# Prompt attention with TensorE's order written out: products of a unit in one run, scores and transposes in turn, exponentials over 1024 columns

## The chip, the cores and the metric

The kernel runs on one core of a Trainium2 chip. The metric is the time of one execution on the device in microseconds (us), the median of several runs. A core has five engines with a queue of instructions each: TensorE (PE in the profile, with its weight loads as PEld), VectorE (DVE), ScalarE (ACT), GpSimd (POOL) and SyncE (SP, which issues most DMAs). An engine works through its queue in order. Waits between engines are semaphores that the framework places from the data dependencies.

## The reference

One inference step of a decoder layer with two kinds of heads, for a prompt of 2048 tokens and for 64 sampled tokens with a paged cache. What matters here is the prompt's forgetting attention, 8 heads of 64 channels, all in float32:

```
L = jnp.cumsum(logf, axis=1).transpose(0, 2, 1)
s = jnp.einsum('bqhd,bkhd->bhqk', q_i, k).astype(jnp.float32) * scale
s = s + L_i[..., :, None] - L[:, :, None, :]
s = jnp.where(k_pos[None, :] <= q_pos[:, None], s, -jnp.inf)
p = jax.nn.softmax(s, axis=-1)
return jnp.einsum('bhqk,bkhd->bqhd', p.astype(v.dtype), v)
```

A query block of 128 rows `qt` (0 to 15) sees the (qt+1)*128 keys up to its own end. The rest of the step (input projection, mLSTM heads, attention over the cache, output projection, layer norms, squared-ReLU MLP) is not touched by the change.

## The kernel before, in words

The kernel is one program of consecutive phases. `phase_b` is the prompt attention; it lies between the input projection with the mLSTM heads and `phase_o`, the output projection. A framework collects the instructions with their dependencies and then decides, from a timeline of its own, in which order they stand on each engine. `tc.issue_after(x)` pins an instruction behind `x` in that order. The order in which the Python code creates instructions is a priority, not a rule.

`phase_b` runs over 64 *units* (h, g): 8 heads, and in each head 8 groups g of two query blocks, qt = 2g and 2g+1; the two blocks are the *halves* i = 0 and 1 of a unit. In step n of the loop the scores of unit n are made and then the values of unit n-1 (`LA = 1`).

`scores` (from L928): for each half the keys are taken in pieces of up to 512 columns. A piece is a *score pair* on PE: two matmuls into one PSUM bank `pS`, with the high part `qh` (L945) and the low part `ql` (L946) of the queries as weights and the keys `ks` streaming. Three banks `pS` take turns. DVE drains the bank into the SBUF tile `S`, adds the forget row `nl` and keeps the maximum (L952); the diagonal 128 columns are drained with the masked row `nd`, which POOL makes (L956). A small DVE reduction makes the row maximum `mx` (L959).

`values` (from L963): ACT takes the exponential in place, one instruction for each 512-column tile, with the row sum in `lp` (L973); DVE adds up `lp` (L974). Then, for every four key blocks, both halves are transposed: up to four 128x128 transposes on PE into a PSUM tile `pt` (L986, three buffers), and a copy of `pt` to SBUF tile `PT` by ACT (L989; half 0, and every second group of half 1) or DVE (L991). I call four such transposes and their copy a *turn*. After the turns of a group come the *value products* of these four key blocks (L995), which accumulate into `po`; a unit has 2g+2 products. In the trace one product leaves two records. At the end `po` is copied out by ACT (L1001) and its second half added by DVE (L1003); after every fourth unit `finish` normalises and stores.

The keys of the next head (`ks`, an ACT and a DVE instruction for each 512 columns, L154 and L157) and the next queries (`qh`, `ql`) are made between the two. `tick`, which feeds other work into some phases, has an infinite pace in this phase and starts nothing. `S` has ten buffers of 512 columns. The two statements of the loop that matter are:

```
sc[n] = scores(Z[h], g)
...
values(Z[h], g, sc.pop(n - LA))
```

Of the kernel before, what the change touches and what calls it, by code (L numbers as in the profile page):

```python
# [10 lines left out]
F32 = mybir.dt.float32  # L11
# [14 lines left out]
S = 2048  # L26
# [26 lines left out]
def body(ctx, tc, I, O, stages):  # L53
# [80 lines left out]
    def tick(us):  # L134

        macc[0] += us
        while macc[1] and macc[0] > macc[2]:
            macc[0] -= macc[2]
            if beside(macc[1][0]) == 0:
                macc[1].pop(0)  # L140
        if not macc[1]:
            macc[0] = 0.0
        acc[0] += us
        while acc[1] is not None and acc[0] > acc[2]:
            acc[0] -= acc[2]
            attend()
# [718 lines left out]
    def phase_b():  # L865
# [58 lines left out]
            split_lo(ql, qn, qh)  # L924
            z["q", g] = qh, ql

        def scores(z, g):

            qh, ql = z.pop(("q", g))
            nl, ks = z["nl"], z["ks"]  # L930
            out = []
            for i in range(2):
                qt = 2 * g + i
                n = (qt + 1) * 128
                qs = slice(i * 128, i * 128 + 128)
                mx = pb.tile([128, 8], F32, name="mx", bufs=6)
                nd = pb.tile([128, 128], F32, name="nd", bufs=3)
                last["POOL"] = G.tensor_tensor(nd, nl[:, qt * 128:n], dmask, op=OP.add)
                st = []
                j = 0  # L940
                for a in range(0, n, 512):
                    b = min(n, a + 512)
                    w = max(b - a, 256)
                    pS = bank()
                    T.matmul(pS[:, :w], qh[:, qs], ks[:, a:a + w], start=True, stop=False)  # L945
                    last["PE"] = T.matmul(pS[:, :w], ql[:, qs], ks[:, a:a + w], start=False, stop=True)  # L946
                    tick(0.42)
                    sp = pb.tile([128, 512], F32, name="S", bufs=10)
                    st.append(sp)
                    e = min(b, qt * 128)  # L950
                    if e > a:
                        last["DVE"] = V.tensor_tensor_reduce(out=sp[:, :e - a], in0=pS[:, :e - a], in1=nl[:, a:e], scale=1.0, scalar=NEG,  # L952
                                               op0=OP.add, op1=OP.max, accum_out=mx[:, j:j + 1])
                        j += 1
                    if b == n:
                        V.tensor_tensor_reduce(out=sp[:, e - a:b - a], in0=pS[:, e - a:b - a], in1=nd, scale=1.0, scalar=NEG,  # L956
                                               op0=OP.add, op1=OP.max, accum_out=mx[:, j:j + 1])
                        j += 1
                V.tensor_reduce(mx[:, 7:8], mx[:, :j], axis=AX.X, op=OP.max, negate=True)  # L959
                out.append((st, mx))  # L960
            return out

        def values(z, g, sc):  # L963

            if z["h"] == 0 and g == 0:
                pad(pb, 64)
            for i, (st, mx) in enumerate(sc):
                qt = 2 * g + i
                n = (qt + 1) * 128
                lp = pb.tile([128, 4], F32, name="lp", bufs=6)  # L970
                for k, sp in enumerate(st):
                    w = min(512, n - k * 512)
                    last["ACT"] = A.activation(sp[:, :w], sp[:, :w], AF.Exp, bias=mx[:, 7:8], accum_out=lp[:, k:k + 1])  # L973
                V.tensor_reduce(z["ls"][:, qt:qt + 1], lp[:, :len(st)], axis=AX.X, op=OP.add)  # L974

            po = ppb.tile([128, 256], F32, name="po", bufs=1)
            nk = 2 * g + 2
            for k0 in range(0, nk, 4):
                PT = pb.tile([128, 4, 256], F32, name="PT", bufs=4)
                for i in range(2):  # L980
                    kk = min(4, 2 * g + i + 1 - k0)
                    if kk <= 0:
                        continue
                    pt = ppb.tile([128, 4, 128], F32, name="pt", bufs=3)
                    for k in range(kk):
                        T.transpose(pt[:, k], sc[i][0][k0 // 4][:, k * 128:(k + 1) * 128], ident)  # L986
                    dst = PT[:, :kk, i * 128:i * 128 + 128]
                    if i == 0 or (k0 // 4) % 2 != 0:
                        A.copy(dst, pt[:, :kk])  # L989
                    else:  # L990
                        V.tensor_copy(dst, pt[:, :kk])  # L991
                for k in range(k0, min(k0 + 4, nk)):
                    q0 = 128 if k == nk - 1 else 0
                    c = (k % 2) * 64
                    last["PE"] = T.matmul(po[c:c + 64, q0:], z["vn"][:, k], PT[:, k - k0, q0:],  # L995
                                          start=(k < 2), stop=(k >= nk - 2), skip_group_check=True)
                tick(0.45 * min(4, nk - k0))
            if g % 4 == 0:
                z["ot"] = pb.tile([64, 1024], F32, name="ot", bufs=2)
            od = z["ot"][:, (g % 4) * 256:(g % 4) * 256 + 256]  # L1000
            A.copy(od, po[0:64])  # L1001
            q0 = 128 if g == 0 else 0
            V.tensor_tensor(od[:, q0:], od[:, q0:], po[64:128, q0:], op=OP.add)  # L1003
            if g % 4 == 3:
                finish(z, g // 4)
# [34 lines left out]
        for n in range(len(units) + LA):  # L1040
            if 10 <= n < 16 and acc[1] is not None:
                attend()
            w2_due[0] += 64 * (n % 8 // 2 + 1) / 150
            while n and len(w2_done) < min(64, w2_due[0]):
                w2_sum()
            if n == 60:
                wo.extend(half_wo(0, q) for q in range(4))
            if n < len(units):
                h, g = units[n]
                sc[n] = scores(Z[h], g)  # L1050
                if h == 0 and g % 2 == 0 and g < 6:
                    keys(Z[0], g // 2 + 1)
                if h < 7:
                    if g == 3:
                        Z[h + 1] = head(h + 1)
                        forget_values(Z[h + 1], 0, S)
                    if g >= 4:
                        keys(Z[h + 1], g - 4)
                if n + 1 < len(units):
                    queries(Z[units[n + 1][0]], units[n + 1][1])  # L1060
            if n >= LA:
                h, g = units[n - LA]
                values(Z[h], g, sc.pop(n - LA))
        es.close()


# [31 lines left out]
    def half_wo(hf, q):  # L1098

        r = raw().rearrange("p (k c) -> p k c", k=2)  # L1100
        SY.dma_start(r, I["w_o2"][hf, q].rearrange("p (k c) -> p k c", k=2))
        return r
# [800 lines left out]
```

## Time and profile before

| | |
|---|---|
| median of 3 runs | 3292.24 us (3286.64 to 3301.8) |
| the profiled execution, its own time | 3288.1 us |
| its span, first to last instruction | 3286.4 us |
| PE busy | 3148.6 us, 96% |
| DVE busy | 2099.1 us, 64% |
| ACT busy | 1500.7 us, 46% |
| POOL busy | 912.9 us, 28% |
| mean granted TensorE clock | 0.984 |

The profile is of one execution. Busy time on PE is the union of the matmuls' records; since matmuls are pipelined, a record goes on after the next one has begun, and a PE that is busy need not be at its peak rate. What an instruction costs its engine in a dense stretch is therefore read from start to start, not from its duration.

### The profile page before, as it was taken

How to read it: one execution, taken by the hardware profiler on the slowest of the kernel's cores; microseconds unless marked ns; L12 is line 12 of the kernel's file. 1: busy time of each engine (PE TensorE's matmuls, PEld its weight loads, DVE VectorE, ACT ScalarE, POOL GpSimd, SP SyncE). 2: the span in 40 equal slices, each digit the busy share in tenths (PEclk: the TensorE clock that was granted, in tenths of full speed). 3: DMA queues.
4: the chain of work that ended last, by engine and by line, in shares of the span. 5: the costliest groups of instructions: out<-in, count | busy, mean ns of one | idle time of the engine just before them, and what ended most of it. 6: DMA issues, size and time to landing. Idle time of an engine off the chain costs nothing.

```text
span 3286.4 us, 58046 instructions
## 1 busy us (share of the span) xinstructions
PE 3148.6 (96%) x21681; PEld 2564.4 (78%) x21681; DVE 2099.1 (64%) x5079; ACT 1500.7 (46%) x2966; POOL 912.9 (28%) x977
## 2 busy tenths in 40 slices
PE   8999998998989999999999999999999999799997
PEld 8998998888856666677677777776777777698895
DVE  6856565355468788644466658656586666856658
ACT  4343343233358888622344345343454444444442
POOL 0121233322324333276433422433333121100000
PEclk9999999999989999999999999999999999999998
DMA  5575766766678675487887878878879666543332
GB/s 186 149 221 177 236 221 216 236 232 198 223 232 226 160 201 136 159 298 253 305 292 273 290 256 298 315 254 327 289 290 343 218 231 211 187 152 119 120 105 100
DMA packets 339698, 734.37 MB, mean 223 GB/s; under 512 B 63640, under 2 KB 177688, under 8 KB 338520
## 3 DMA queue, kind: packets, MB, share of 16 engines
q1 hardware_dynamic: 252856, 416.71, 39.6%
q0 software_dynamic: 83520, 304.12, 26.6%
q10 hardware_dynamic: 3040, 9.83, 0.8%
q8 instruction: 171, 2.80, 0.3%
q14 instruction: 111, 0.91, 0.1%
HBM read 677.71 MB, written 86.38 MB: 233 GB/s over the span
## 4 chain that ended last, share of the span: by engine, by line
PE 45%; DVE 3%; DMA 3%; issue 1%; POOL 1%; ACT 1%; another core or an unknown queue 0%; DVEq 0%; POOLq 0%; ACTq 0%; SPq 0%
PE ph L162 7%; PE ph L163 7%; PE ph L164 7%; PE py L162 6%; PE py L164 5%; PE py L163 5%; PE sO L1759 3%; PE sQ L1647 2%; DMA vt<-cache_v,idxV 1%; DVE wl L157 1%; PE sT L1716 1%; DVE y L1323 1%; DMA kT<-cache_k,idxK 0%; PE pw L163 0%; PE pw L164 0%
## 5 line engine op out<-in xcount | busy, mean ns | idle before, releaser
L157 DVE TENSOR_TENSOR wl<-wr,wh 128x1024 fp32r<-128x1024 f32 x364 | 445.6, 1226 | 376.3 <-ACT wh L154 341.0
L154 ACT ACTIVATE wh<-wr 128x1024 fp32r<-128x1024 f32 x364 | 382.6, 1054 | 321.8 <-PE ph L163 131.1
L162 PE MATMUL ph<-x1h,wh 128*128 128x512 f32 (+1 forms) x1280 | 455.8, 356 | 0.8 <-DVE x1l L157 0.5
L163 PE MATMUL ph<-x1l,wh 128*128 128x512 f32 (+1 forms) x1280 | 453.9, 355 | 0.0
L1624 POOL DMA_INDIRECT kT<-cache_k,idxK x256 | 273.7, 1069 | 640.0 <-PE sQ L1647 578.0
L164 PE MATMUL ph<-x1h,wl 128*128 128x512 f32 (+1 forms) x1280 | 451.3, 354 | 0.0
L162 PE MATMUL py<-wh,hh 128*128 128x512 f32 x896 | 356.8, 400 | 5.9 <-DVE y L1323 2.5
L163 PE MATMUL py<-wl,hh 128*128 128x512 f32 x896 | 351.6, 392 | 0.3 <-issue 0.3
L164 PE MATMUL py<-wh,hl 128*128 128x512 f32 x896 | 349.6, 393 | 1.3 <-DVE hl L157 1.0
L1323 DVE TENSOR_TENSOR y<-y,py 128x512 f32<-128x512 f32 x416 | 280.3, 682 | 69.0 <-PE py L164 55.7
L162 PE MATMUL pm<-xh,whi 128*128 128x256 f32 (+1 forms) x1024 | 301.7, 295 | 1.3 <-issue 0.8
L163 PE MATMUL pm<-xl,whi 128*128 128x256 f32 (+1 forms) x1024 | 297.6, 291 | 2.3 <-issue 2.2
L164 PE MATMUL pm<-xh,wlo 128*128 128x256 f32 (+1 forms) x1024 | 296.8, 290 | 2.8 <-issue 2.8
L162 PEld LDWEIGHTS ph<-x1h,wh 128*128 128x128 f32 x1280 | 241.3, 189 | 40.9 <-issue 7.8
L1735 POOL DMA_INDIRECT vt<-cache_v,idxV x164 | 175.3, 1069 | 340.5 <-PE sO L1759 272.6
L163 PEld LDWEIGHTS ph<-x1l,wh 128*128 128x128 f32 x1280 | 241.5, 189 | 34.2 <-issue 3.7
L164 PEld LDWEIGHTS ph<-x1h,wl 128*128 128x128 f32 x1280 | 241.0, 189 | 34.1 <-issue 3.7
L162 PE MATMUL pm<-whi,xh 128*128 128x256 f32 (+2 forms) x816 | 238.7, 293 | 9.2 <-ACT whi L154 8.3
L163 PE MATMUL pm<-wlo,xh 128*128 128x256 f32 (+2 forms) x816 | 233.9, 287 | 1.6 <-issue 1.0
L164 PE MATMUL pm<-whi,xl 128*128 128x256 f32 (+2 forms) x816 | 233.5, 286 | 0.9 <-issue 0.8
L973 ACT ACTIVATE S<-S,mx 128x512 f32<-128x512 f32 (+2 forms) x320 | 207.8, 653 | 18.2 <-DVE mx L959 15.8
L162 PEld LDWEIGHTS py<-wh,hh 128*128 128x128 f32 x896 | 168.3, 188 | 55.5 <-issue 14.0
(371 smaller groups left out, 6810.5 us busy)
## 6 DMA issues: line engine op xcount, KB each, us to landing
wr<-w SPq DMA_DIRECT2D x224, 512.0 KB
wr<-dw SPq DMA_DIRECT2D x128, 512.0 KB
wra<-w_in SPq DMA_DIRECT2D x104, 512.0 KB
dw<-w POOLq DMA_DIRECT2D x48, 512.0 KB
Rb<-dR SPq DMA_DIRECT2D x128, 128.0 KB
xn<-xp_t SPq DMA_DIRECT2D x16, 512.0 KB
kn<-k_prompt SPq DMA_DIRECT2D x64, 128.0 KB
qn<-dq SPq DMA_DIRECT2D x128, 64.0 KB
```

Source lines behind the costliest of these rows:

```text
L154: last["ACT"] = A.activation(dst, src, AF.Copy, scale=scale)
L157: r = (eng or V).tensor_tensor(dst, src, hi.bitcast(F32), op=OP.subtract)
L162: T.matmul(ps, wh, xh, start=first, stop=False, skip_group_check=shared)
L163: T.matmul(ps, wh, xl, start=False, stop=False, skip_group_check=shared)
L164: last["PE"] = T.matmul(ps, wl, xh, start=False, stop=stop, skip_group_check=shared)
L973: last["ACT"] = A.activation(sp[:, :w], sp[:, :w], AF.Exp, bias=mx[:, 7:8], accum_out=lp[:, k:k + 1])
L1323: V.tensor_tensor(y, y, ps, op=op)
L1624: G.indirect_dma_start(out=piece(n), out_offset=None, in_=ck, in_offset=IO(ap=idxK[:, b, j // 2, j % 2:j % 2 + 1], axis=0))
L1647: r = T.matmul(pq[h4 * 32:h4 * 32 + 32, hg].rearrange("p (k c) -> p k c", k=2), z["qb"][:, hd], kv, start=(db == 0), stop=(db == 1), skip_ ...
L1716: T.transpose(p[:, f], z["U"][u][:, hg, f].rearrange("p k t -> p (k t)"), ident)
L1735: G.indirect_dma_start(out=vt.rearrange("p f c -> p (f c)"), out_offset=None, in_=cv, in_offset=IO(ap=idxV[:, b, (kt % 4) * 4 + kt // 4, f ...
L1759: after_ = T.matmul(po[r:r + 32], z["PT"][:, hg, 2 * f + g, pg].rearrange("p h q -> p (h q)"), vts[f][:, g, hg * 256:(hg + 1) * 256], star ...
```

## The change

The change touches `phase_b` alone.

- A helper `pe` issues every matmul and transpose of the phase behind the one before it, so that PE's order is the order in which the code makes them.
- `scores` becomes a generator that stops after each score pair. The maximum, the exponentials and the sum of a half now follow directly on its last pair.
- `S` gets 1024 columns and 8 buffers, and one exponential covers up to 1024 columns.
- `values` is cut in two. `turns` is a generator that makes one turn (transposes and copy) at a time, first all of half 0, then all of half 1. `products` makes all value products of a unit in one run.
- The loop takes a turn of unit n-1 and a score pair of unit n alternately until both are used up. Then come the keys and queries, and then the products of unit n-1.
- The two `tick` calls go.

```diff
+        def pe(f, *a, **k):
+
+            with tc.issue_after(last["PE"].ins):
+                last["PE"] = f(*a, **k)
+
-        def scores(z, g):
+        def scores(z, g, out):
...
-                    T.matmul(pS[:, :w], qh[:, qs], ks[:, a:a + w], start=True, stop=False)
-                    last["PE"] = T.matmul(pS[:, :w], ql[:, qs], ks[:, a:a + w], start=False, stop=True)
-                    tick(0.42)
-                    sp = pb.tile([128, 512], F32, name="S", bufs=10)
-                    st.append(sp)
+                    pe(T.matmul, pS[:, :w], qh[:, qs], ks[:, a:a + w], start=True, stop=False)
+                    pe(T.matmul, pS[:, :w], ql[:, qs], ks[:, a:a + w], start=False, stop=True)
+                    if a % 1024 == 0:
+                        st.append(pb.tile([128, 1024], F32, name="S", bufs=8))
+                    sp = st[-1][:, a % 1024:a % 1024 + 512]
...
-                V.tensor_reduce(mx[:, 7:8], mx[:, :j], axis=AX.X, op=OP.max, negate=True)
-                out.append((st, mx))
-            return out
-
-        def values(z, g, sc):
+                        V.tensor_reduce(mx[:, 7:8], mx[:, :j], axis=AX.X, op=OP.max, negate=True)
+                        lp = pb.tile([128, 2], F32, name="lp", bufs=6)
+                        for k, sp in enumerate(st):
+                            w = min(1024, n - k * 1024)
+                            last["ACT"] = A.activation(sp[:, :w], sp[:, :w], AF.Exp, bias=mx[:, 7:8], accum_out=lp[:, k:k + 1])
+                        V.tensor_reduce(z["ls"][:, qt:qt + 1], lp[:, :len(st)], axis=AX.X, op=OP.add)
+                        out.append(st)
+                    yield
+
+        def turns(z, g, sc, PT):
...
-            for i, (st, mx) in enumerate(sc):
-                qt = 2 * g + i
-                n = (qt + 1) * 128
-                lp = pb.tile([128, 4], F32, name="lp", bufs=6)
-                for k, sp in enumerate(st):
-                    w = min(512, n - k * 512)
-                    last["ACT"] = A.activation(sp[:, :w], sp[:, :w], AF.Exp, bias=mx[:, 7:8], accum_out=lp[:, k:k + 1])
-                V.tensor_reduce(z["ls"][:, qt:qt + 1], lp[:, :len(st)], axis=AX.X, op=OP.add)
-
-            po = ppb.tile([128, 256], F32, name="po", bufs=1)
             nk = 2 * g + 2
-            for k0 in range(0, nk, 4):
-                PT = pb.tile([128, 4, 256], F32, name="PT", bufs=4)
-                for i in range(2):
+            for i in range(2):
+                for k0 in range(0, nk, 4):
+                    if i == 0:
+                        PT.append(pb.tile([128, 4, 256], F32, name="PT", bufs=4))
                     kk = min(4, 2 * g + i + 1 - k0)
-                    if kk <= 0:
-                        continue
                     pt = ppb.tile([128, 4, 128], F32, name="pt", bufs=3)
                     for k in range(kk):
-                        T.transpose(pt[:, k], sc[i][0][k0 // 4][:, k * 128:(k + 1) * 128], ident)
-                    dst = PT[:, :kk, i * 128:i * 128 + 128]
+                        c = k0 % 8 * 128 + k * 128
+                        pe(T.transpose, pt[:, k], sc[i][k0 // 8][:, c:c + 128], ident)
+                    dst = PT[k0 // 4][:, :kk, i * 128:i * 128 + 128]
...
-                for k in range(k0, min(k0 + 4, nk)):
-                    q0 = 128 if k == nk - 1 else 0
-                    c = (k % 2) * 64
-                    last["PE"] = T.matmul(po[c:c + 64, q0:], z["vn"][:, k], PT[:, k - k0, q0:],
-                                          start=(k < 2), stop=(k >= nk - 2), skip_group_check=True)
-                tick(0.45 * min(4, nk - k0))
+                    yield
+
+        def products(z, g, PT):
+
+            po = ppb.tile([128, 256], F32, name="po", bufs=1)
+            nk = 2 * g + 2
+            for k in range(nk):
+                q0 = 128 if k == nk - 1 else 0
+                c = (k % 2) * 64
+                pe(T.matmul, po[c:c + 64, q0:], z["vn"][:, k], PT[k // 4][:, k % 4, q0:],
+                   start=(k < 2), stop=(k >= nk - 2), skip_group_check=True)
...
+            S_, T_ = iter(()), iter(())
             if n < len(units):
                 h, g = units[n]
-                sc[n] = scores(Z[h], g)
+                sc[n] = []
+                S_ = scores(Z[h], g, sc[n])
+            if n >= LA:
+                hv, gv = units[n - LA]
+                PT = []
+                T_ = turns(Z[hv], gv, sc.pop(n - LA), PT)
+            while True:
+                more = [next(x, 1) for x in (T_, S_)]
+                if more == [1, 1]:
+                    break
+            if n < len(units):
...
             if n >= LA:
-                h, g = units[n - LA]
-                values(Z[h], g, sc.pop(n - LA))
+                products(Z[hv], gv, PT)
```

More of the change, by code (lines that the diff above doesn't have):

```diff
@@ L925, in queries @@
             z["q", g] = qh, ql
-        def scores(z, g):
+        def pe(f, *a, **k):
+            with tc.issue_after(last["PE"].ins):
+                last["PE"] = f(*a, **k)
+        def scores(z, g, out):
             qh, ql = z.pop(("q", g))
             nl, ks = z["nl"], z["ks"]
-            out = []
             for i in range(2):
```

## The prediction

> **What bounds the kernel now.** I read the page first, then the windows of the phase head by head, the groups of the phase by line, and then the timelines of PE, ACT and DVE.
>
> ```profile
> span 3286.4 us, 58046 instructions
> PE 3148.6 (96%) x21681; PEld 2564.4 (78%) x21681; DVE 2099.1 (64%) x5079; ACT 1500.7 (46%) x2966; POOL 912.9 (28%) x977
> PEclk9999999999989999999999999999999999999998
> ```
>
> PE is busy almost throughout. The phase runs from 927.7 to 1364.8 us; its heads, cut where the last products of each are copied out, are (columns: window, length, then busy time of PE, PEld, DVE, ACT, POOL, granted clock, DMA):
>
> ```profile
> core 0: us, PE busy (x) PEld busy (x) DVE busy (x) ACT busy (x) POOL busy (x), PEclk, DMA share, GB/s
> 927.70:1002.20 74.50, 64.89 (x391) 42.73 (x392) 58.80 (x236) 57.19 (x162) 28.50 (x47) 0.92 0.90 286
> 1002.20:1055.50 53.30, 52.62 (x363) 36.66 (x362) 43.12 (x174) 45.36 (x128) 22.26 (x32) 1.00 0.74 195
> ...
> 1267.20:1317.90 50.70, 50.70 (x357) 35.82 (x358) 40.63 (x167) 43.66 (x124) 17.84 (x27) 1.00 0.64 132
> 1317.90:1364.80 46.90, 46.17 (x333) 32.92 (x333) 30.33 (x114) 35.39 (x98) 8.58 (x13) 1.00 0.18 52
> ```
>
> The six heads between 1002.2 and 1317.9 take 52.6 us each (315.7 / 6). PE is 97% to 100% busy in them, DVE and ACT 80% to 86%. So PE bounds the phase, but busy PE hides slow starts. What its work costs at its densest follows from the counts and from one stretch of its timeline:
>
> ```profile
> L973 ACT ACTIVATE S<-S,mx 128x512 f32<-128x512 f32 (+2 forms) x320 | 207.8, 653 | 18.2 <-DVE mx L959 15.8 <-DVE ls L974 1.8
> L986 PE MATMUL pt<-ident,S 128*128 128x128 f32 x1088 | 162.0, 278 | 7.0 <-ACT S L973 3.4 <-DVE PT L991 1.8 <-ACT PT L989 0.5
> L995 PE MATMUL po<-PT,vn 128*64 128x256 f32 (+1 forms) x1152 | 149.5, 378 | 2.5 <-DVE ot L1003 1.8 <-ACT qh L154 0.6
> L945 PE MATMUL pS<-ks,qh 128*128 128x512 f32 (+2 forms) x320 | 135.7, 429 | 7.7 <-ACT qh L154 4.0 <-DVE mx L952 1.7 <-DVE mx L956 0.7
> ```
>
> ```profile
> 1153.72 0.49 PE L986 MATMUL pt<-ident,S 128*128 128x128 f32 x3
> 1154.14 1.95 PE L995 MATMUL po<-PT,vn 128*64 128x256 f32 x16
> 1156.02 0.66 PE L986 MATMUL pt<-ident,S 128*128 128x128 f32 x4
> 1156.43 0.48 PE L945 MATMUL pS<-ks,qh 128*128 128x512 f32 x1
> 1156.75 0.40 PE L946 MATMUL pS<-ks,ql 128*128 128x512 f32 x1
> 1157.07 1.08 PE L995 MATMUL po<-PT,vn 128*64 128x256 f32 x8
> 1158.09 0.33 PE L986 MATMUL pt<-ident,S 128*128 128x128 f32 x1
> 1158.17 0.48 PE L945 MATMUL pS<-ks,qh 128*128 128x512 f32 x1
> 1158.49 0.40 PE L946 MATMUL pS<-ks,ql 128*128 128x512 f32 x1
> 1158.72 0.40 PE L945 MATMUL pS<-ks,qh 128*128 128x512 f32 x1
> 1158.96 0.39 PE L946 MATMUL pS<-ks,ql 128*128 128x512 f32 x1
> 1159.19 0.38 PE L986 MATMUL pt<-ident,S 128*128 128x128 f32 x2
> ```
>
> Read from start to start. A transpose costs 0.109 us (two in 0.38, each 0.27 long). 16 records (8 products) last from 1154.14 to 1156.02, 8 records (4 products) from 1157.07 to 1158.09: 0.86 us for four more, 0.215 per product, and 0.16 over per run. Two more costs stand at a run's edges: a score's second matmul is followed by a product after 0.32 us (1156.75) but by a score after 0.23 (1158.49), and four transposes behind a run take 0.41 (1156.02) instead of 4 x 0.109 less the 0.08 by which a score starts early behind a transpose. So **each run of products costs 0.30 us** beside its products. A score pair of 512 columns costs 0.47 behind a pair (1158.72 to 1159.19), and 0.55 behind a transpose, which then itself costs 0.08 less: 0.47 again.
>
> **The change, part by part.**
>
> *Products in one run.* In the instruction order of the built programs the products stand in 114 runs before and 64 after. 50 x 0.30 = 15.0 us less on PE. PE is the path here, so it counts in full, unless PE waits longer.
>
> *Scores alternating with transposes.* By the rows above a pair costs 0.47 either way: nothing, from both sides.
>
> The whole sum of PE: 1088 transposes x 0.109 = 118.6; 512 products x 0.215 and 64 of half the columns = 117.1; 224 pairs of 512 columns x 0.47, 32 of 384 and 64 of 256 by their columns = 131.6; together 367.3, or 45.9 a head. With 114 x 0.30 it is 50.2 a head, with 64 x 0.30 it is 48.3. The six middle heads take 52.6, so PE waits 2.4 us a head now.
>
> *Exponentials of 1024.* ACT, start to start:
>
> ```profile
> 1196.30 1.66 ACT L154 ACTIVATE ks<-kn 128x512 fp32r<-128x512 f32 x3
> 1197.86 0.41 ACT L154 ACTIVATE qh<-qn 128x256 fp32r<-128x256 f32 x1
> ...
> 1199.95 0.71 ACT L973 ACTIVATE S<-S,mx 128x512 f32<-128x512 f32 x1
> ...
> 1200.66 0.71 ACT L973 ACTIVATE S<-S,mx 128x512 f32<-128x512 f32 x1
> ...
> 1203.12 0.39 ACT L973 ACTIVATE S<-S,mx 128x128 f32<-128x128 f32 x1
> ...
> 1203.50 0.58 ACT L989 COPY PT<-pt 128x512 f32<-128x512 f32 x1
> 1203.97 0.51 ACT L973 ACTIVATE S<-S,mx 128x256 f32<-128x256 f32 x1
> ```
>
> With its accumulator read, an exponential takes 0.71 for 512 columns and 0.38 for 128, so 0.86 ns a column and, extended, 1.15 for 1024. Two of 512 cost 1.42. The count goes from 320 to 192: 128 x 0.27 = 35 us less on ACT. ACT does not bound, so this is worth nothing by itself. It also makes the first transposes of a tile wait 0.44 longer for a whole tile. DVE's work stays; POOL's and SP's instructions stay, only shifted among each other, and I cost that at nothing within some us. `S` grows from 5120 to 8192 columns, which ends waits of DVE's drains for transposes; DVE has 20% to spare.
>
> *The written order.* Now a transpose that waits for its exponential holds up every score pair and product behind it on PE, and DVE's drains wait for those scores. Before, the framework let other work pass. I followed one middle head by hand through the new order of PE, ACT and DVE with the costs above, a copy of a turn at 0.47 on ACT (1203.50 to 1203.97), `qh` at 0.32, `ks` at 0.52, and on DVE:
>
> ```profile
> 1058.10 0.68 DVE L952 CUSTOM_DVE_ANT_0 S<-pS,nl 128x512 f32<-128x512 f32 x1
> ...
> 1058.70 0.29 DVE L956 CUSTOM_DVE_ANT_0 S<-pS,nd 128x128 f32<-128x128 f32 x1
> ...
> 1058.98 0.68 DVE L991 COPY PT<-pt 128x512 f32<-128x512 f32 x1
> 1059.58 0.68 DVE L952 CUSTOM_DVE_ANT_0 S<-pS,nl 128x512 f32<-128x512 f32 x1
> ```
>
> (a drain 0.60, the masked drain 0.21, a copy 0.60). Two places make PE wait.
>
> The head's end, unit g=7 to the next g=0. After the last score pair of g=7, PE has the products of g=6, 0.30 + 13 x 0.215 + 0.11 = 3.2 us, then three turns and two small pairs, 1.8: the fourth turn is due at 5.0 and needs a free `pt`. ACT has, in this order: the rest of an exponential (0.75), a short copy (0.25), `qh` (0.32), three `ks` (1.56), two exponentials of 1024 (2.30), the copy of `po` (0.25): 5.4. Only then come the copies of the turns, at 0.47, with `qh`, `ks` and two small exponentials (1.7 together) between them. The eight turns end at 9.8 instead of 7.1: 2.7 us of wait.
>
> The small units g=0 to 3. From a half's last pair to its transposes stand the pair's own end (0.40), a drain (0.60), the masked drain (0.29), the maximum (0.15) and the exponential (0.6 to 1.15): 2.0 to 2.6 us, and DVE has the sum into `ot` (0.45) and copies in its queue between. PE has only 0.8 to 2 us of other work there. The walk gives 1.0 before the products of g=0 and 1.2 after them, 0.3 in g=1, 0.7 in g=2 and 3: 3.2 us.
>
> Units 4 to 7 come out without a wait: behind a unit's last score stand 1.9 to 3.2 us of products and half a unit of turns. Sum 5.9 us a head in place of 2.4. So a head takes 48.3 + 5.9 = 54.2 in place of 52.6, +1.6, over the seven later heads about **+10 us**. The first head (74.5 us, DMA 0.90, clock 0.92) waits for loads, which stay: 0, with 5 us either way.
>
> The profiled execution took 3288.1 us, 1.7 more than its span; it lies 4.1 under the median of 3292.2. Its sum is 3288 + 10 = 3298; against the median I forecast **3302 us**. A walk by hand can miss 2 us a head, so this case spans 3288 to 3316.
>
> **The rivals.**
>
> *PE waits no more than before.* If DVE and ACT run ahead of my walk, 2.4 us a head stay and the 15 us are kept: 3277 (3262 to 3287). For it: ACT loses 35 us of work. Against it: the waits at g=0 to 3 are latencies, not load.
>
> *The exponentials hold up the turns in large units too.* ACT takes instructions in order; where the exponentials of half 1 stand before the first copies of the next unit, and end later than three turns (2.7 us) after the products, all three `pt` fill. In units 4 to 6 this costs one exponential, 1.15, 24 times: 28 us on top, 3330 (3317 to 3345). It decides at the point where mx is late by 1 us against my walk; late loads of `qn` or `kn` would do that. Against it: 15% to 20% idle ACT before, more after.
>
> *The clock drops at the head's end.* There PE gets 23 transposes in a row, with waits between them. Rows of before that are nearest:
>
> ```profile
> 1356.95 1.09 PE L986 MATMUL pt<-ident,S 128*128 128x128 f32 x8
> 1358.48 1.50 PE L986 MATMUL pt<-ident,S 128*128 128x128 f32 x12 [0.44 <-DVE ls L974]
> ```
>
> 20 transposes in 3 us, and the last head's granted clock is 1.00. If 23 transposes and 2.7 us of waits (5.2 us) were followed by as long a stretch at half speed, 2.6 us would be lost at seven ends: 18 us, 3320. [...]
>
> *The order isn't what was written*: excluded by the 64 runs, but for 2%; 3292.
>
> **How the numbers follow.** About 0.5% (16.5 us) is what a measurement of this kernel tells from no change, so "same" is 3275.8 to 3308.7. Chances: forecast 0.46, no more waits 0.22, exponentials 0.22, clock 0.08, order 0.02. Faster: half of the second case lies under 3275.8, with some of the first for an error in the walk, 0.16. Slower: the third case, most of the clock's and nearly a quarter of the first, 0.40. Same: 0.44. The range leaves out a tenth at each end: 3270, in the middle of the lower case, to 3334, in the middle of the upper one. As cases of both signs hold most of the chance, the forecast's own range is 3288 to 3316.
>
> **What would show it.** Right: products in 64 runs with PE's dense costs unchanged; ACT's busy time in the phase some 35 us lower; PE waits for L988's copies at each head's end, 2 to 3 us, and for exponentials and drains in g=0 to 3; middle heads of 54 us. Wrong: middle heads under 51 us, or PE waits in g=4 to 6, or a granted clock under 0.97 in a middle head.

## The result, and the profile after

The changed kernel takes **3312.59 us** (median of 5 runs, 3308.13 to 3328.4) against 3288.33 us of the kernel before on the same chip. The ratio is 1.0087, 95% interval [1.0063, 1.0110]: 24 us slower. The forecast of 3302 us was too low by 10.6 us; the time lies inside the forecast's own range of 3288 to 3316. The profiled execution took 3310.28 us, 22.2 more than that of before.

First the page of the changed kernel: the span, the busy times, and the granted clock in 40 slices.

```profile
span 3308.6 us, 57761 instructions
PE 3140.7 (95%) x21681; PEld 2571.3 (78%) x21681; DVE 2098.1 (63%) x5079; ACT 1471.3 (44%) x2710; POOL 919.6 (28%) x977
PEclk9999999999989999999999999999999999899998
```

PE is busy for 8 us less and ACT for 29 us less, and yet the span is longer: the time went into waiting. The windows of the changed kernel, cut as before where the last products of each head are copied out (window, length, busy time of PE, PEld, DVE, ACT, POOL, granted clock, DMA):

```profile
core 0: us, PE busy (x) PEld busy (x) DVE busy (x) ACT busy (x) POOL busy (x), PEclk, DMA share, GB/s
923.50:997.00 73.50, 58.33 (x366) 41.20 (x366) 51.62 (x192) 46.70 (x109) 20.60 (x36) 0.85 0.82 256
997.00:1052.50 55.50, 50.60 (x362) 36.71 (x362) 44.22 (x172) 41.57 (x97) 23.09 (x34) 1.00 0.72 207
1052.50:1108.00 55.50, 50.61 (x362) 36.69 (x362) 43.43 (x172) 41.60 (x97) 19.95 (x30) 1.00 0.78 172
1108.00:1166.50 58.50, 52.11 (x362) 37.98 (x362) 44.65 (x172) 41.71 (x97) 17.94 (x29) 0.97 0.61 158
1166.50:1223.50 57.00, 52.03 (x362) 37.70 (x361) 44.33 (x172) 41.56 (x97) 18.57 (x30) 0.97 0.67 164
...
1332.00:1385.20 53.20, 49.37 (x356) 35.96 (x354) 38.12 (x154) 37.30 (x85) 13.05 (x20) 1.00 0.29 68
```

The phase takes 461.6 us in place of 437.0. Its 24.6 us are the whole loss: the phase starts 4.1 us earlier, and what comes behind it takes 1.7 us more. For each head I take the counts of matmuls in its window by the prediction's prices (0.109 for a transpose, 0.215 for a product, 0.47 for a pair, 0.30 for a run); what the window is longer than that I call waiting (it also holds what a halved clock adds):

| head | before: length, dense, waiting | after: length, dense, waiting |
|---|---|---|
| 0 | 74.4, 55.8, 18.6 | 73.5, 48.9, 24.5 |
| 1 | 53.4, 50.9, 2.5 | 55.5, 48.4, 7.1 |
| 2 | 53.5, 51.3, 2.1 | 55.5, 48.4, 7.1 |
| 3 | 52.1, 49.3, 2.8 | 58.5, 48.4, 10.1 |
| 4 | 53.8, 51.3, 2.4 | 57.0, 48.4, 8.7 |
| 5 | 52.3, 49.3, 3.1 | 54.6, 48.4, 6.2 |
| 6 | 50.7, 49.2, 1.5 | 53.8, 48.4, 5.4 |
| 7 | 46.8, 44.7, 2.1 | 53.3, 47.8, 5.6 |

By these prices dense work fell by 15 us, and waiting rose by 39.6. (Before, the framework had also pulled work of each next head into the one ahead of it, hence the 55.8 at the start and the 44.7 at the end; in the written order each head holds just its own.) The groups of the phase name the new waits (busy, mean ns, then idle before and what ended it):

```profile
L930 PE MATMUL pt<-ident,S 128*128 128x128 f32 x1088 | 178.0, 282 | 38.6 <-ACT S L967 25.8 <-ACT PT L988 11.3 <-ACT ot L1005 1.4
L967 ACT ACTIVATE S<-S,mx 128x1024 f32<-128x1024 f32 (+2 forms) x192 | 171.8, 897 | 29.4 <-DVE mx L963 29.0
L930 PE MATMUL po<-PT,vn 128*64 128x256 f32 (+1 forms) x1152 | 138.4, 373 | 6.8 <-ACT qh L154 4.8 <-DVE PT L990 1.3
```

Transposes waited 7.0 us before and 38.6 now: 25.8 for exponentials, 11.3 for ACT's copies. The exponentials themselves wait for the row maximum (29.0 of their 29.4 us): in the small units ACT isn't late from load, the chain ahead of it is long.

**The small units.** PE's timeline of the changed kernel around unit g=1 of head 2:

```profile
1053.35 0.39 PE L930 MATMUL pS<-ks,ql 128*128 128x512 f32 x1
1054.42 0.62 PE L930 MATMUL po<-PT,vn 128*64 128x256 f32 x4 [0.69 <-ACT qh L154]
1056.20 0.55 PE L930 MATMUL pt<-ident,S 128*128 128x128 f32 x3 [1.17 <-ACT S L967]
1056.51 0.48 PE L930 MATMUL pS<-ks,qh 128*128 128x512 f32 x1
1056.82 0.40 PE L930 MATMUL pS<-ks,ql 128*128 128x512 f32 x1
```

The last pair of g=1 ends at 1053.74. Two products of g=0 are all that the written order has left (the profile names `qh` for their wait; the last to come is DVE's copy of the turn), then the transposes of g=1 wait for their exponential. Measured as distance from start to start above the dense one, heads 1 and 2 each show 0.76 us before the products of g=0, 1.23 behind them, 0.18 in g=1, 1.36 before the transposes of g=2, 0.27 in g=4 and 5, and 2.19 at the head's end: 6.0, and 1.1 in pieces under 0.06 us.

**The head's end**, on ACT and on PE:

```profile
1038.81 1.03 ACT L967 ACTIVATE S<-S,mx 128x896 f32<-128x896 f32 x1
...
1040.41 1.67 ACT L154 ACTIVATE ks<-kn 128x512 fp32r<-128x512 f32 x3
1041.97 1.15 ACT L967 ACTIVATE S<-S,mx 128x1024 f32<-128x1024 f32 x1
1043.11 1.15 ACT L967 ACTIVATE S<-S,mx 128x1024 f32<-128x1024 f32 x1
...
1044.49 1.07 ACT L988 COPY PT<-pt 128x512 f32<-128x512 f32 x2
```

```profile
1043.71 0.60 PE L930 MATMUL pt<-ident,S 128*128 128x128 f32 x4
1045.14 1.14 PE L930 MATMUL pt<-ident,S 128*128 128x128 f32 x7 [0.82 <-ACT PT L988]
1046.79 1.10 PE L930 MATMUL pt<-ident,S 128*128 128x128 f32 x8 [0.52 <-ACT PT L988]
1048.18 0.66 PE L930 MATMUL pt<-ident,S 128*128 128x128 f32 x4 [0.29 <-ACT PT L988]
1048.77 3.67 PE L930 MATMUL po<-PT,vn 128*64 128x256 f32 x32
```

After three turns the three `pt` are full; the first copy stands at 1044.49 on ACT behind three `ks` and the exponentials, and PE then follows the copies, one by one.

**Head 3 is 3 us longer than head 2**, and here is the same place of it on PE:

```profile
1108.81 0.40 PE L930 MATMUL pS<-ks,ql 128*128 128x512 f32 x1
1109.90 0.62 PE L930 MATMUL po<-PT,vn 128*64 128x256 f32 x4 [0.69 <-ACT qh L154]
1112.54 0.90 PE L930 MATMUL pt<-ident,S 128*128 128x128 f32 x3 [2.02 <-ACT S L967]
1113.10 0.78 PE L930 MATMUL pS<-ks,qh 128*128 128x512 f32 x1
1113.67 0.63 PE L930 MATMUL pS<-ks,ql 128*128 128x512 f32 x1
```

PE waits 0.85 us longer than in head 2, and then runs at half speed: from a pair's first to its second matmul 0.57 us instead of 0.31. What differs ahead of it is one instruction on DVE, `ql`, and what POOL does beside it (DVE first, then POOL; head 2 in the first row of each, head 3 in the second):

```profile
1054.92 0.42 DVE L157 TENSOR_TENSOR ql<-qn,qh 128x256 fp32r<-128x256 f32 x1
...
1110.40 1.28 DVE L157 TENSOR_TENSOR ql<-qn,qh 128x256 fp32r<-128x256 f32 x1
```

```profile
1055.25 2.51 POOL L1025 TENSOR_TENSOR ot<-ot,rl 64x512 f32<-64x512 f32 x2 [9.76 <-DMA rl<-drl]
...
1110.11 2.69 POOL L1025 TENSOR_TENSOR ot<-ot,rl 64x512 f32<-64x512 f32 x2 [9.15 <-DMA rl<-drl]
```

`ql` takes 0.42 where it begins before POOL's product, and 1.28 when POOL's normalising product of the head before has begun 0.29 us earlier; the maximum, the exponential and the transposes behind it are late by as much.

### The profile page after: what moved, and what is told of

It reads as the page before. It is cut to its first block, busy times and chain, and to the rows that moved or that the text cites. A ratio compares the mean times of both kernels' runs of the same rounds, so it can differ in the third digit from the quotient of the medians.

```text
span 3308.6 us, 57761 instructions
## 1 busy us (share of the span) xinstructions
PE 3140.7 (95%) x21681; PEld 2571.3 (78%) x21681; DVE 2098.1 (63%) x5079; ACT 1471.3 (44%) x2710; POOL 919.6 (28%) x977
## 3 DMA queue, kind: packets, MB, share of 16 engines
q1 hardware_dynamic: 252856, 416.71, 39.6%
## 4 chain that ended last, share of the span: by engine, by line
PE 45%; DMA 3%; DVE 3%; issue 1%; POOL 1%; ACT 1%; another core or an unknown queue 0%; DVEq 0%; POOLq 0%; ACTq 0%; SPq 0%
PE ph L162 7%; PE ph L163 7%; PE ph L164 7%; PE py L162 5%; PE py L164 5%; PE py L163 5%; PE sO L1773 3%; PE sQ L1661 2%; DMA vt<-cache_v,idxV 2%; DVE wl L157 1%; PE sT L1730 1%; DVE y L1337 1%; POOL kT L1638 0%; PE pw L163 0%; PE pw L164 0%
## 5 line engine op out<-in xcount | busy, mean ns | idle before, releaser
L930 PE MATMUL pt<-ident,S 128*128 128x128 f32 x1088 | 178.0, 282 | 38.6 <-ACT S L967 25.8
```

What stands on the lines that cost most here:

```text
L930: last["PE"] = f(*a, **k)
```

## The experiments

Theory A: PE waits because the written order leaves it nothing to do while the chain drain, maximum, exponential, copy runs. B: the wide exponentials are the loss. D: whatever wait is taken away comes back at the next place. E: writing the order costs in the large units too. Medians of before were 3286.1 us for the first four runs, 3283.9 for the next four, 3282.4 for the last four, each on one chip. The ratios are against the runs of before on that chip, and lie up to 0.002 beside the quotient of the two medians.

**The order set free.** In `pe`:

```diff
-            with tc.issue_after(last["PE"].ins):
-                last["PE"] = f(*a, **k)
+            last["PE"] = f(*a, **k)
```

> The changed kernel without the pinned order of TensorE: the helper pe issues its instruction without issue_after, so that the framework may let other work pass; all else stays (alternating generators, exponentials of 1024, products created in one piece). The built order has 111 runs of products. Theory A (the loss is waits that the written order lays on TensorE, 6.9 us a head in place of 2.4, and 6 us more in the first head): the waits fall back to 2 to 3 us a head, the runs cost 14 us again, and the time is that of before, 3288 within 8 us. Theory B (the loss comes from the exponentials of 1024 columns, which let the first transposes of a tile wait longer): nothing changes, 3305 to 3320.

Measured: 3290.19 us, ratio 1.0013 [0.9994, 1.0032]; the products stand in 111 runs. So nearly all the loss is the written order. The timeline of PE in this kernel shows what the framework does at the place where the changed kernel waits (start of head 2):

```profile
1061.60 0.98 PE L929 MATMUL pt<-ident,S 128*128 128x128 f32 x7
1062.34 0.48 PE L929 MATMUL pS<-ks,qh 128*128 128x512 f32 x1
...
1062.89 0.28 PE L929 MATMUL pS<-ks,qh 128*128 128x256 f32 x1
...
1063.56 0.39 PE L929 MATMUL pS<-ks,qh 128*128 128x512 f32 x1
...
1064.66 0.65 PE L929 MATMUL po<-PT,vn 128*64 128x256 f32 x4
```

Three pairs stand ahead of the two products of g=0 (4 records). The one of 256 columns is of g=2, whose scores the code makes only behind these products: the framework has pulled them forward, and no row has a wait. Its heads 1 to 6 wait 2.7 us each on average (16.2 in all), and pay 50.2 us of dense work each for the extra runs: 1.8 us more than the written order, and 4.7 less waiting.

**Exponentials of 512 in the changed kernel**:

```diff
-                        for k, sp in enumerate(st):
-                            w = min(1024, n - k * 1024)
-                            last["ACT"] = A.activation(sp[:, :w], sp[:, :w], AF.Exp, ...)
+                        for k in range(0, n, 512):
+                            sp = st[k // 1024][:, k % 1024:k % 1024 + min(512, n - k)]
+                            last["ACT"] = A.activation(sp, sp, AF.Exp, ...)
```

> The changed kernel with exponentials of 512 columns again (two instructions on the same 1024-column tile). Theory A: the four small units have no exponential over 1024 columns and few over 512, so their waits of 3.5 us a head stay; ScalarE gets 35 us more work, which lengthens its queue at each head's end by up to 1 us: 3308 to 3325. Theory B: the waits shrink by 0.4 us for every tile and the time goes to about 3290.

Measured: 3328.98 us, 1.0124 [1.0095, 1.0152]. B falls: narrow exponentials do not take the loss away. Going by the two ratios they make it 12 us larger; the two intervals overlap, but the traces agree, with 60 us of waiting in heads 1 to 6 in place of 45. At the end of head 1 PE waits for the copies at once 2.48 us, where the changed kernel has 0.82, 0.52 and 0.29:

```profile
1045.18 3.23 PE L930 MATMUL pt<-ident,S 128*128 128x128 f32 x13 [2.48 <-ACT PT L988]
```

**Exponentials of 1024 in the kernel before**, nothing else:

```diff
-                    sp = pb.tile([128, 512], F32, name="S", bufs=10)
-                    st.append(sp)
+                    if a % 1024 == 0:
+                        st.append(pb.tile([128, 1024], F32, name="S", bufs=8))
+                    sp = st[-1][:, a % 1024:a % 1024 + 512]
...
-                    w = min(512, n - k * 512)
+                    w = min(1024, n - k * 1024)
```

> The kernel before with the 1024-column tiles (8 buffers) and exponentials of up to 1024 columns alone; order, products and ticks as before. Theory A: 3280 to 3292, since ScalarE loses 35 us of work but does not bound and the framework keeps TensorE fed. Theory B: slower than before by 15 to 25 us, 3303 to 3313.

Measured: 3282.71 us, 0.9992 [0.9972, 1.0012]. ACT's saving is worth nothing where the order is free, as the prediction had it; under the written order, where PE stands still until ACT has come, the run above puts it at about 12 us.

**A unit more of distance** between scores and turns (`LA = 2`):

> The changed kernel with LA = 2: in step n the transposes and products of unit n-2 stand beside the scores of unit n, so that a whole unit lies between a score and the transposes that need its exponential; TensorE's order is still written, exponentials still 1024 wide, still 8 tiles S. Theory A: the waits at g=0 to 3 (3.5 us a head) go, those for the copies at the head's end (2.2 us) stay or move to the next units, and with the long waits the drops of the clock in two heads go too: 3280 to 3290, TensorE's waits 2 to 3.5 us a head. Theory B: the exponentials stay, the time stays at 3305 to 3320. Third case: 8 tiles are too few for three units, and DVE's drains wait for tiles in g=5 to 7: 3310 or more with waits there.

Measured: 3328.55 us, 1.0130 [1.0107, 1.0153]. Priced unit by unit, heads 1 to 7 wait 0.4, 0.2 and 0.8 us in g=0 to 2, in place of 0.8, 1.5 and 1.5 in heads 1 and 2 of the changed kernel: they shrink, as A said. New ones come: 1.4 us in g=3 (0.1 in the changed kernel), 1.0 in g=4 (0.3), 0.65 in g=5 (0.3), and 1.6 to 3.2 in the step of g=6, where the turns of an older large unit have only small pairs beside them; in heads 2, 3 and 5 that step loses 4.5 to 6.4 us:

```profile
1045.84 0.33 PE L930 MATMUL pt<-ident,S 128*128 128x128 f32 x1 [1.62 <-ACT PT L988]
```

The first head's waits grow from 24.5 to 37.1 us. D.

**A pair before a turn** instead of a turn before a pair:

```diff
-                more = [next(x, 1) for x in (T_, S_)]
+                more = [next(x, 1) for x in (S_, T_)]
```

> The changed kernel with the two generators in the other order: in each round of the loop the score pair comes first and the turn after it; order still written, all else stays. Theory A (latency: a small unit's transposes stand too close behind the scores that they need): each of the waits at g=0 to 2 gets up to one score pair, 0.47 us, of cover, 1.0 to 1.4 us a head, the head's end stays: 3300 to 3306. Theory D (throughput: ScalarE and VectorE in their fixed order are what is late, so that TensorE's waits only move): no change, 3309 to 3320.

Measured: 3315.07 us, 1.0077 [1.0048, 1.0106]. At the two places of 1.23 and 1.36 us some 0.5 us each is left, but now a unit's products stand right behind its last turn, whose copy they need. Head 2, before the products of g=0:

```profile
1062.35 0.62 PE L930 MATMUL po<-PT,vn 128*64 128x256 f32 x4 [1.59 <-issue]
```

At the products of g=1 to 3 another 1.4 us a head is added. D.

**Copies shared evenly** between ACT and DVE:

```diff
-                    if i == 0 or (k0 // 4) % 2 != 0:
+                    if (k0 // 4 + i) % 2 != 0:
```

> The changed kernel with the copies of the turns shared out evenly: half 0 gives its even turns to VectorE and the odd ones to ScalarE, half 1 the other way round (before: all of half 0 and the odd ones of half 1 on ScalarE). Theory A: at the head's end the first turn no longer waits behind ScalarE's keys and exponentials, the wait of 2.2 us falls to about 1, the small units stay: 3302 to 3308. Theory D: VectorE, with 8 more copies a head, 5 us, becomes the one that is late, and TensorE waits for its drains: 3312 to 3330.

Measured: 3306.99 us, 1.0059 [1.0041, 1.0077]. The head's end falls from 2.2 to 2.0 only, and the wait before g=0 falls from 0.76 to 0.12, but the wait behind it rises from 1.23 to 1.7, and to 2.5 to 3.1 in four heads. There `ql` runs into POOL's product again (PE, then DVE, start of head 1):

```profile
1000.04 0.55 PE L930 MATMUL pt<-ident,S 128*128 128x128 f32 x3 [2.96 <-ACT S L967]
```

```profile
997.48 1.69 DVE L157 TENSOR_TENSOR ql<-qn,qh 128x256 fp32r<-128x256 f32 x1
```

Behind that wait of 2.96 us PE is slower: the four transposes from 1001.09 take 1.06 us, where those at the same place of the changed kernel (1001.59) take 0.60.

**Both edits together**, pair first and copies shared:

> The edits of e5 and e6 together. Theory A: the two add up, 3290 to 3298. Theory D: 3310 or more.

Measured: 3315.08 us, 1.0090 [1.0059, 1.0121]: no better than either.

**The order written for units 4 to 7 only**: `pe` pins a matmul only while the unit that it belongs to has g >= 4.

```diff
+            if not pinned[0]:
+                f(*a, **k)
+                return
             with tc.issue_after(last["PE"].ins):
...
-                more = [next(x, 1) for x in (T_, S_)]
+                more = []
+                for x, of in ((T_, n - LA), (S_, n)):
+                    pinned[0] = of % 8 >= 4
+                    more.append(next(x, 1))
...
+                pinned[0] = gv >= 4
                 products(Z[hv], gv, PT)
```

> The changed kernel with the written order only for the scores, turns and products of units with g of 4 and more; those of g=0 to 3 are free to be placed by the framework. The built order has 92 runs of products. Theory A: the 3.5 us a head at g=0 to 3 go nearly all, the first head loses part of its 6 us, 28 more runs cost 8 us, and the head's end gets small units to fill it: 3280 to 3292. If the written order of the large units costs too (theory E), the time stays above 3300.

Measured: 3290.55 us, 1.0018 [1.0002, 1.0033], 92 runs. E falls: large units can be written at the price of the free order, but nothing is gained either. The waits of the large units' transposes are nearly gone too, those for copies at the head's end among them (0.6 us in all, where the changed kernel has 11.3):

```profile
L933 PE MATMUL pt<-ident,S 128*128 128x128 f32 x800 | 120.9, 275 | 2.6 <-ACT S L970 2.0 <-ACT PT L991 0.6
```

Yet three `ks` stand on ACT at the end of head 1 as in the changed kernel, with two exponentials of 1024 behind them and the first copies of the last turns at 1045.73:

```profile
1040.96 1.66 ACT L154 ACTIVATE ks<-kn 128x512 fp32r<-128x512 f32 x3
```

PE has score pairs of the next head's small units to do in the meantime, and does not wait.

**The order written for units 0 to 3 only**, the complement (`< 4` in place of `>= 4`, twice):

> The complement of the kernel whose order was written for units g=4 to 7 only: here PE's order is written for the scores, turns and products of units g=0 to 3 of every head, and the scheduler places those of g=4 to 7 (nothing is left out). Theory A (the loss lies in the written order of the small units, where one unit's work is shorter than the chain through drain, exponential and copy): nearly the whole loss is here, 3304 to 3314, ratio 1.006 to 1.009, waits of 2 to 3 us a head in g=0 to 3 as in the changed kernel. Theory F (the loss needs the whole chain of order: with large units free, the scheduler pulls their scores forward into the small units' gaps): 3290 to 3298, ratio 1.001 to 1.004, waits in g=0 to 3 under 1.5 us a head.

Measured: 3323.59 us, 1.0117 [1.0091, 1.0144]. The loss comes with the small units' written order, as A has it, and is above A's range; F is out. The groups of the phase keep the pinned matmuls apart by their line, L933; L930 are the free ones:

```profile
L933 PE MATMUL pt<-ident,S 128*128 128x128 f32 x288 | 50.0, 289 | 22.0 <-ACT S L970 22.0
L930 PE MATMUL pt<-ident,S 128*128 128x128 f32 x800 | 123.5, 280 | 10.7 <-ACT PT L991 10.7
```

These 288 transposes, a quarter of all, wait 22 us for exponentials. The 800 of the large units, free to be placed, still wait 10.7 us for copies: with the small units written, the wait at the head's end comes back. The kernel loses more than the changed one, since it pays for the waits (4.7 to 10.8 us in heads 1 to 6) and, at 15 runs in each of these heads, does not get the runs' 15 us.

**Key splits two units earlier**, in three kernels. In the loop:

```diff
-                    if g == 3:
+                    if g == (1 if h else 3):
...
-                    if g >= 4:
-                        keys(Z[h + 1], g - 4)
+                    if (2 if h else 4) <= g < (6 if h else 8):
+                        keys(Z[h + 1], g - (2 if h else 4))
```

in the changed kernel:

> The changed kernel, with the next head's key splits issued two units earlier from the second head on (for heads 1 to 6 the loads and ks of the next head behind units 2 to 5 instead of 4 to 7; nothing is left out). In the changed kernel PE waits 2.2 us at each head's end, while the copies of the last unit's turns stand in ACT's queue behind three ks splits, a qh and the wide exponentials. Theory A (the written order turns the clump at the head's end into a wait): the 2.2 us fall to about 0.7 in six heads, nothing new elsewhere, -9 us: 3301 to 3306, ratio 1.004 to 1.006. Theory D (the waits only move): the splits now stand before the copies of units 3 to 6, PE waits 0.3 to 0.5 us more in each of them, and the time is within 4 us of the changed kernel: 3309 to 3316, ratio 1.007 to 1.010.

in the kernel before with exponentials of 1024:

> The kernel before with the 1024-column exponentials and the next head's key splits two units earlier from the second head on (nothing is left out). Control for the run of the changed kernel with early splits, and a try at a version faster than both. In the kernel before PE waits 1.5 to 3.1 us in a middle head. Theory A: the scheduler already fills the head's end with other work, so the early splits are worth under 1 us a head: 3278 to 3285, ratio 0.998 to 1.000. Theory D (ACT's queue holds turns there too): 1.5 us a head are won: 3270 to 3276, ratio 0.9955 to 0.9975.

and in the kernel written for units 4 to 7 only:

> The changed kernel with its order written for units g=4 to 7 only (that took 3290.6 us), and the next head's key splits two units earlier from the second head on (nothing is left out). The written end of the head is kept, the small units are free. Theory A: the wait at the head's end falls by about 1.5 us in six heads and nothing takes its place, -6 to -9 us: 3280 to 3285, ratio 0.998 to 1.000. Theory D: the wait moves to units 3 to 6, 3287 to 3293, ratio 1.000 to 1.002.

Measured: 3308.67 us, 1.0083 [1.0062, 1.0104]; 3282.74, 1.0005 [0.9989, 1.0020]; 3289.28, 1.0022 [1.0010, 1.0033]. None of them tested what it was made for, though the times would fit D. On ACT, three `ks` stand at the end of head 1 as they did:

```profile
1038.79 1.66 ACT L154 ACTIVATE ks<-kn 128x512 fp32r<-128x512 f32 x3
```

Only PE's order is written; on ACT the code's order is a priority, and the framework still put the splits off until the next head's scores were near. That the clump of `ks` makes the head's end wait is therefore not shown by taking it away. The kernel written for units 4 to 7 shows that the clump alone does not: it has the same three `ks`, and next to no wait for copies. None of the twelve is faster than before by more than its interval.

## Why the prediction was right or wrong

*Products in one run*: right as far as is known. There are 64 runs, and the prices hold in the changed kernel: 16 products take 3.60 us from start to start (1048.77 to 1052.37), four transposes behind a run 0.41 (1042.31 to 1042.72). The 15 us are these prices times 50 fewer runs; no run changed the runs of products alone.

*Exponentials*: right. ACT's busy time in the phase is 31 us lower (331.5 in place of 362.6) for 35 forecast, and by itself that is worth nothing.

*Scores alternating with transposes, S, POOL and SP at nothing*: the pairs cost the same (0.55 us start to start behind a transpose, as before: 1036.90 to 1037.45). POOL at nothing was the step with a hole in it; see below.

*The walk through a middle head*: right in place, and nearly so in size. Walked 1.0, 1.2, 0.3, 0.7, none in units 4 to 7, and 2.7 at the end, together 5.9; found 0.76, 1.23, 0.18, 1.36, 0.27 and 2.19, together 6.0, with small pieces 7.1. That the places add up so well is partly luck: g=2 took twice what was walked, and the head's end 0.5 us less. In heads 1 and 2 that is 55.5 us in place of 54.2.

*What the walk could not see*: it was one head, undisturbed, and it was taken six times. Heads 3 and 4 wait 10.1 and 8.7. In them POOL's product `ot`, started by the landing of a DMA (`rl`), falls on DVE's `ql` and adds 0.85 and 0.62 us to the wait at g=1; the fourth `ks` of head 3's end waits 0.96 us for its load on ACT, and PE's last wait there is 1.37 in place of 0.29; and the clock is halved for 3.4 us in each, about 1.7 us lost (58.5 us at 0.97). The kernel before has the same hitch, and larger. In its head 5:

```profile
1238.30 1.85 DVE L157 TENSOR_TENSOR ql<-qn,qh 128x256 fp32r<-128x256 f32 x1
```

PE has work throughout there, and that head waits 3.1 us in all. A free order let other matmuls pass the hitch; the written one handed it to PE. The six middle heads together wait 30.2 us more, against 6 x 3.5 = 21 forecast.

*The first head at nothing, within 5 us*: a mis-sized term. Its waiting rose by 5.9 us. The prediction said that it waits for loads, which stay; they stay, but what waits behind them changed. In the first head of the changed kernel, on ACT and on PE:

```profile
934.37 0.63 ACT L154 ACTIVATE ks<-kn 128x512 fp32r<-128x512 f32 x1 [3.75 <-DMA kn<-k_prompt]
```

```profile
935.66 0.90 PE L930 MATMUL pt<-ident,S 128*128 128x128 f32 x3 [1.91 <-ACT S L967]
...
938.77 1.12 PE L930 MATMUL pt<-ident,S 128*128 128x128 f32 x4 [1.36 <-ACT S L967]
...
943.94 0.66 PE L930 MATMUL pt<-ident,S 128*128 128x128 f32 x4 [1.30 <-ACT S L967]
...
957.58 0.66 PE L930 MATMUL pt<-ident,S 128*128 128x128 f32 x4 [2.75 <-ACT S L967]
```

An exponential queues on ACT behind a split that waits for its load, and PE's whole queue waits for that exponential. So it is for the first wait, for the second (a `qh` that waits 0.52 us) and for the last (a `ks` with 2.10 and a `qh` with 0.69); the third is the 1.30 that heads 1 and 2 have as well. The clock has a share in it: it is at half for 21.5 us of this head, where before it was for 11.4 (0.85 and 0.92 over the head). By the prices 6.2 and 3.1 us of work were done in these stretches, and half speed adds as much again, so that I estimate 3 of the 5.9 us as the clock's. This part isn't the written order's alone: with the order free the first head waits 26.8 us (in an execution of 3297.5, 7 above that kernel's median), while the kernel before with wide exponentials has 19.3. The new order of the code, free or pinned, costs there, and no run took the first head apart further.

*The sum.* Waiting +39.6 (first head 5.9, six middle heads 30.2, last head 3.5; an estimated 6.4 of it is the halved clock, in heads 0, 3 and 4) against +24.5 forecast; dense work -15 as forecast. (Seven heads of +1.6 are 11.2, which the prediction put at about 10.) The 15 us of difference, less 2.4 outside the phase, make the 12 us by which the profiled execution passed the 3298 that were summed for it.

*The rivals.* That PE waits no more than before is excluded by the table. That exponentials hold up turns in units 4 to 6 did not happen: the changed kernel waits 0.27 there. (ACT was at 83% to 88% of the middle heads before by the windows, a little more than the 80% to 86% that the prediction read.) The dropped clock was a right fear at the wrong place. The changed kernel's windows, in columns as above, of the half-speed stretch in head 3 and of the head's end with its 23 transposes:

```profile
1112.20:1115.80 3.60, 3.26 (x13) 2.89 (x14) 1.62 (x6) 1.48 (x5) 2.27 (x4) 0.53 0.99 207
...
1042.30:1052.40 10.10, 8.47 (x69) 6.00 (x69) 5.68 (x20) 6.90 (x17) 1.77 (x4) 1.00 0.80 214
```

Transposes in a row, with waits of 0.82, 0.52 and 0.29 us between them, leave the clock at 1.00. It falls where PE stood still for 0.69 + 2.02 us within 3.7 (head 3) and for 0.69 + 1.79 (head 4): PE was busy for 0.92 of the 3.4 us from 1108.9 to 1112.3, and for 1.39 of those from 1166.9 to 1170.3. In this trace the clock changes whole multiples of 3.41 us apart (it falls at 958.7, 1112.3 and 1170.3); on that grid the stretch from 1044.0 to 1047.5 holds nothing but transposes and 1.3 us of waits, PE is busy for 2.06 us of it, and the clock stays at 1.00. The slow stretches in heads 3 and 4 last 3.4 us each; the waits of 0.69 + 1.17 us in heads 1 and 2 leave the clock at 1.00.

## What to carry to other kernels

A written instruction order turned a hitch of another engine into idle time of the engine that is pinned where that engine had too little other work in between: here in the small units (pinned alone, their transposes wait 22.0 us), and not in the large ones (2.6 us). Before writing one, take for each step the chain that the next step needs (here 2.0 to 2.6 us of drain, maximum and exponential, by the prediction's costs) and see whether the pinned engine has that much work of its own in between; where a step is shorter than the chain, as in the small units here, leave the order free or bring work in from further away. And cost a stage that waits for loads by what will stand behind those waits, not by the waits that it has now.

## What the runs showed of the hardware

`ql` on DVE takes 0.42 us (the median of its 64 instructions, before and after). Where it begins inside POOL's product `ot` (about 1.3 us), it ends 0.28 to 0.38 us after that product, or after the POOL product that follows it, at all 14 such places of the two kernels: 1.28 and 1.05 us in heads 3 and 4 of the changed kernel, 0.42 at 1225.89, 0.13 us ahead of the product's end, and up to 1.85 before. With the copies shared evenly one such `ql` took 1.69 (997.48). Why DVE is late there the traces do not show. In heads 3 and 4 of the changed kernel PE's granted clock was 0.50 for 3.41 us at a time (from 1112.31 and 1170.33), around the end of waits of 0.69 + 2.02 and 0.69 + 1.79 us; it stayed at 1.00 through 23 transposes in a row, with 1.6 us of waits among them (1042.3 to 1052.4). The changed kernel's runs spread with it: at a mean clock of 0.978 and 0.979 they took 3328 and 3325 us, at 0.980 to 0.981 3308 to 3313.
